# A hybrid attention and recurrence block: second copies of the values made on GpSimd, weight steps ahead of evictions, and the row of positions in free tiles

## The chip, the core and the metric

The kernel runs on one core of a Trainium2 chip. A core has five engines that run their own instruction streams and meet only at semaphores: TensorE (PE in the profile, its weight loads PEld) multiplies into PSUM, VectorE (DVE) and ScalarE (ACT) work elementwise on SBUF and PSUM, GpSimd (POOL) works on SBUF and issues DMAs, and SyncE (SP) issues DMAs. The metric is the device time of one execution in microseconds; less is better.

## What is computed

One block of a decoder over 1024 tokens of width 1024, all in float32: an RMS norm modulated by a condition vector, one input projection whose columns feed two branches, an attention over a sliding window of 128 with a learned sink per head, a gated linear recurrence behind a short convolution, the merge of both, an output projection and a final norm.

```python
h = rmsnorm(x, norm_g[l]) * (1.0 + scale[:, None, :]) + shift[:, None, :]
proj = h @ w_in[l]
q, k, v, g_attn, xr, g_rnn, m_attn, m_rnn = jnp.split(proj, SPLIT_POINTS, axis=-1)
q = partial_rope(q.reshape(B, S, N_HEADS, HEAD_DIM), positions)
k = partial_rope(k.reshape(B, S, N_KV_HEADS, HEAD_DIM), positions)
v = v.reshape(B, S, N_KV_HEADS, HEAD_DIM)
y_attn = sliding_window_attention_with_sinks(q, k, v, attn_sinks[l]) * jax.nn.silu(g_attn)
xr = causal_depthwise_conv(xr, conv_w[l], conv_b[l])
y_rnn = rg_lru(xr, positions, ...) * jax.nn.silu(g_rnn)
merged = (jax.nn.sigmoid(m_attn) * (y_attn @ w_attn_proj[l])
          + jax.nn.sigmoid(m_rnn) * (y_rnn @ w_rnn_proj[l]))
x = x + gate[:, None, :] * (merged @ w_out[l])
return rmsnorm(x, final_g)
```

## The kernel before

**Products.** Every float32 operand is split into a high part and a remainder, each in a form that TensorE multiplies at full rate, and a product is the sum of three (high by high, remainder by high, high by remainder). ScalarE makes the high part of a weight (`wh`, `cast`, line 104) and VectorE the remainder (`wl`, `rest`, line 110 or, with a scale, 112). The projection's columns are worked off in pairs of 128-column chunks by a scheme of Strassen's kind with seven products: `class Pair` holds one such pair, `product` (line 707) is one product of twelve matmuls, and a product fills one slot of the order.

**Order.** The instruction order of all engines is the order in which the Python code emits it. `Pair.place` enters a pair's steps into the list `fixed` by slot: loads of weights, their sums (`ws`, line 729), high parts and remainders ahead of the products that use them, and behind the products the evictions of the PSUM banks `bk`: copies by ScalarE (`u`, `p`, `bk`, lines 756 to 759), joins by VectorE (`c` or `xr`, line 767) and the sinks (`tanh_sinks`: a tanh on ScalarE, line 810, and for the SiLU gates a multiplication on VectorE, line 815). Two helpers enter steps: `at_slot` appends to a slot's list, `ahead` puts in front of what is there. The weight steps of a pair begin two slots before its first product, where the pair before it is being evicted. They are entered with `ahead` where the pair before is one of the queries (in `Q`), otherwise with `at_slot`, thus behind that pair's evictions. `run` walks over the slots, and `background` fills in the steps of the recurrence (`waiting`), whose scan is line 1064.

**The gate row.** `gate_row` (line 1092) reduces eight 128x1024 tiles of a weight with VectorE. A ninth tile of the same two buffers (`stage`) takes the row of positions, spread over 128 partitions, and line 1108 makes a reset mask (`rbig`) of it. The four tiles `wq` are not used until the output weights are prepared, behind the gate row.

**Attention.** The loop over `u` runs 35 iterations, each with one step of a software pipeline: scores of `u`, softmax of `u - 1`, transposes (`pt`), split (`phc` on ScalarE, `plc` on VectorE) and masks of `u - 2`, and the product with the values of `u - 3`. `masks` makes `cm` on GpSimd with two instructions, one for the upper 64 partitions from `phc`, one for the lower 64 from `plc` (line 1372); the last two matmuls of `values` read it in the next iteration (line 1386). Between these, `piece` emits a few matmuls of the rest of the projection and later of the recurrence branch's output projection (`rp`, line 175), so that TensorE has work while a softmax is under way. `sink` fills a column of the next score tile on GpSimd (`p`, line 1301).

**Values.** `load_v(m)` fills two tiles for two iterations, `vb` and `vd`, whose 128 partitions hold the values of 64 positions twice (for `vb` the second copy is one block on). Each is loaded in two halves by GpSimd's queue: four DMAs of 128 KB. It is called in `values` of an even iteration, two tiles ahead. The same queue carries the stores of the merge gates (`smr_d`), issued right behind their tanh. SyncE's queue carries the other loads of this stage, among them the recurrence branch's results `yh` and `yl`.

Of the kernel before, what the change touches and what calls it, by code (L numbers as in the profile page):

```python
# [12 lines left out]
F32 = mybir.dt.float32  # L13
F32R = mybir.dt.float32r
U32 = mybir.dt.uint32
I32 = mybir.dt.int32
BF16 = mybir.dt.bfloat16
AF = mybir.ActivationFunctionType
ALU = mybir.AluOpType
# [3 lines left out]
P = 128  # L23
S = 1024
D = 1024
KC = 8
# [26 lines left out]
def tile_hybrid_block(ctx, tc, x, x_t, pk, rows, posr, posi, c_row, w_ss, w_gate, w_main, w_v,  # L53
# [733 lines left out]
                "C21": lambda s: rope_b(s, 0, q_d[g]), "C22": (blk, lambda s: rope_b(  # L787
                    s, 1, q_d[g])), "late": 11}

    behind = []  # L790

    def store(dst, src):

# [9 lines left out]
    def tanh_sinks(dst, silu):  # L803
        def steps(j, th):
            def sink(s):
                t = {}

                def f1():
                    t["t"] = blk()
                    A.activation(t["t"], s(), AF.Tanh, scale=0.5)  # L810
                    if not silu:
                        dma(dst[j][:, SL[th]], t["t"], G)

                def f2():
                    V.scalar_tensor_tensor(out=t["t"], in0=t["t"], scalar=1.0, in1=s(),
                                           op0=ALU.add, op1=ALU.mult)
                    store(dst[j][:, SL[th]], t["t"])

                return [("A", 0.62, 0, f1)] + ([("D", 0, 0.69, f2)] if silu else [])
            return sink  # L820
        return {"C11": steps(0, 0), "C12": (blk, steps(0, 1)), "C21": steps(1, 0),
                "C22": (blk, steps(1, 1))}

    def place(pairs):
        for i, p in enumerate(pairs):
            p.place(7 * i, (i + len(pairs) + 1) % 2, i == len(pairs) - 1,
                    ahead if i and pairs[i - 1] in Q else at_slot)

    def run(pairs, extra):

# [261 lines left out]
    def gate_row():  # L1092
# [1 line left out]
        t = {}  # L1094

        def load(c):
            t[c] = gm.tile([P, D], F32 if c < KC else I32, tag="stage", name="wg", bufs=2)
            dma(t[c][:], w_gate[c * P:(c + 1) * P, :] if c < KC else posi.to_broadcast([P, S]))

        def start():  # L1100
            t["c"] = gm.tile([P, D], F32, name="cb")
# [3 lines left out]

        def step(c):
            if c == KC:
                V.tensor_scalar(out=rbig[:], in0=t[c][:], scalar1=0.0, scalar2=200.0,
                                op0=ALU.is_equal, op1=ALU.mult)
            else:  # L1110
                V.scalar_tensor_tensor(out=t[c][:], in0=t[c][:], scalar=0.25, in1=t["c"][:],
                                       op0=ALU.mult, op1=ALU.mult,
                                       accum_out=gate_bc[:, 0, c:c + 1])
# [43 lines left out]
        for c in range(KC + 1):  # L1157
            waiting[2].append([("D", 0, 1.28, lambda c=c: step(c))])
            if c + 2 <= KC:
                waiting[2].extend([slots(1), [("S", 0, 0, lambda c=c: load(c + 2))]])  # L1160
            waiting[2].extend(todo[c:c + 1] or [slots(1)])
        waiting[2].extend([[("D", 0, 0.1, out_row)], slots(6),
                           [("S", 0, 0, lambda: dma(
# [76 lines left out]

    at_ctx, psx_ctx = ExitStack(), ExitStack()
    at = psx = None
    U = {}

    def open_attn():
        nonlocal at, psx
# [35 lines left out]
    def load_v(m):  # L1282
        g, i0 = m // 4, m % 4 * 4
        vb = at.tile([P, 4, P], F32R, tag="vb", name="vb", bufs=3)
        vd = at.tile([P, 4, P], F32R, tag="vd", name="vd", bufs=3)
        for e in range(2):
            half = slice(64 * e, 64 * e + 64)
            dma(vb[half], vs_d[g][:, i0 + e:i0 + e + 4, :], G)
            dma(vd[half], dv_d[g][:, i0 + 2:i0 + 6, :], G)
        U["v", m] = vb, vd  # L1290

    def sink(u):
# [85 lines left out]
    def values(u):  # L1378
# [5 lines left out]
        for i, (b, m, h) in enumerate(prods):  # L1384
# [1 line left out]
            W["pe"] = T.matmul(pv[:, js, :], b[:, u % 2 * 2 + h, :], m[:, js, :],  # L1386
                               start=(i == 0), stop=(i >= len(prods) - 2),
                               skip_group_check=True)
        if u % 2 == 0 and u // 2 + 2 < 16:
            load_v(u // 2 + 2)  # L1390
        U["pv", u] = [pv[:].rearrange("p (h a) (e q) -> p a e h q", h=2, e=2)]

    def join_a(u):
# [284 lines left out]
    for u in range(32 + 3):  # L1678
# [31 lines left out]
            sink(u + 1)()  # L1710
        if 2 <= u < 34:
            masks(u - 2)
        if "hpool" in W:
            for f in low:
                f()
# [430 lines left out]
```

## Time and profile before

| what | before |
|---|---|
| runs | 905.7, 909.52, 909.77 us; median 909.52 |
| profiled execution | 906.86 us, of which the span 905.1 us |
| granted clock of TensorE | 0.998 of full speed |
| HBM read and written | 127.37 MB and 55.28 MB |

The span is the time from the first to the last instruction of one profiled execution; all positions below are microseconds from its start. A row of a timeline has the start, the length, the engine, the line and the operation, `out<-in` by the program's names. A matmul's length includes its way through the array, so that the rows of consecutive matmuls overlap. Idle time of an engine stands in brackets, with the instruction that ended it.

### The profile page before, as it was taken

What the parts mean: (1) busy time and instruction counts of PE and PEld (TensorE: products, weight loads), DVE (VectorE), ACT (ScalarE), POOL (GpSimd) and SP (SyncE); (2) the same over time, 40 slices, a digit from 0 to 9 for tenths busy, and PEclk for the clock granted to TensorE, in tenths of its full rate; (3) what the DMA queues carried; (4) which work ended last, traced back from release to release, by engine and by line L of the source; (5) the groups of instructions that cost most, each with busy time, mean ns of one, the idle gap of its engine ahead of it and who ended that gap; (6) DMA issues with size and microseconds to landing.
All of it is one profiled execution on the core that took longest, in us unless ns stands there. A gap on an engine that the chain in (4) does not pass through costs nothing.

```text
span 905.1 us, 12954 instructions
## 1 busy us (share of the span) xinstructions
PE 882.7 (98%) x4235; PEld 737.6 (81%) x4235; DVE 721.7 (80%) x1166; ACT 553.7 (61%) x1099; POOL 183.4 (20%) x309
## 2 busy tenths in 40 slices
PE   5999999999999999999999999998999999999997
PEld 3879888888888788878887888887888888888886
DVE  7988798888669974986698476898999846779875
ACT  6754675554566746674777685877888631114555
POOL 0130232210110000000100003565665421310002
PEclk9999999999999999999999999999999999999999
DMA  9951885972534451344244246899889369869314
GB/s 350 414 187 63 292 248 194 311 246 93 181 134 139 149 200 34 137 148 170 104 164 169 82 152 208 280 330 296 222 229 259 122 209 328 297 253 325 141 47 185
DMA packets 99445, 183.12 MB, mean 202 GB/s; under 512 B 31329, under 2 KB 44129, under 8 KB 99378
## 3 DMA queue, kind: packets, MB, share of 16 engines
q1 hardware_dynamic: 86912, 144.52, 47.1%
q0 software_dynamic: 12176, 37.47, 12.5%
q8 instruction: 33, 0.54, 0.2%
q10 hardware_dynamic: 290, 0.32, 0.1%
q14 instruction: 34, 0.28, 0.1%
HBM read 127.37 MB, written 55.28 MB: 202 GB/s over the span
## 4 chain that ended last, share of the span: by engine, by line
PE 70%; DMA 11%; issue 8%; DVE 5%; ACT 4%; POOL 2%; SPq 0%; DVEq 0%; POOLq 0%; ACTq 0%
PE bk L707 39%; PE bo L1918 8%; PE rp L175 7%; PE pgate L1003 5%; DMA yl<-yl_d 3%; PE pmain L175 2%; PE s_ps L1317 2%; DMA r<-w_main 2%; PE pv L1386 2%; DMA wq<-w_out 2%; DMA hl<-yl_d 1%; DMA wq_d<-wq 1%; PE pt L1354 1%; PE bk L175 1%; DVE wl L110 1%
## 5 line engine op out<-in xcount | busy, mean ns | idle before, releaser
L707 PE MATMUL bk<-nh,wl 128*128 128x512 f32 x368 | 143.7, 390 | 0.4 <-DVE wl L110 0.4
L707 PE MATMUL bk<-nh,wh 128*128 128x512 f32 x368 | 143.3, 390 | 0.0
L707 PE MATMUL bk<-nl,wh 128*128 128x512 f32 x368 | 143.2, 389 | 0.0
L707 PEld LDWEIGHTS bk<-nh,wl 128*128 128x128 f32 x368 | 69.1, 188 | 16.1 <-DVE wl L110 1.9
L110 DVE TENSOR_TENSOR wl<-r,wh 128x512 fp32r<-128x512 f32 x112 | 81.4, 740 | 0.0
L707 PEld LDWEIGHTS bk<-nh,wh 128*128 128x128 f32 x368 | 69.1, 188 | 14.4
L707 PEld LDWEIGHTS bk<-nl,wh 128*128 128x128 f32 x368 | 69.1, 188 | 14.1
L60 POOL DMA_DIRECT2D wq_d<-wq x32 | 21.9, 684 | 270.4 <-DVE wq L1191 255.4
L104 ACT CAST wh<-r 128x512 fp32r<-128x512 f32 x112 | 68.0, 617 | 9.0 <-DMA r<-w_ap 6.3
L707 PE MATMUL bk<-hh,wl 128*128 128x512 f32 x184 | 71.7, 390 | 0.1
L707 PE MATMUL bk<-hh,wh 128*128 128x512 f32 x184 | 71.6, 389 | 0.0
L707 PE MATMUL bk<-hl,wh 128*128 128x512 f32 x184 | 71.6, 389 | 0.0
L110 DVE TENSOR_TENSOR wl<-ws,wh 128x512 fp32r<-128x512 f32 x80 | 54.5, 684 | 4.2 <-ACT wh L104 4.2
L1340 ACT ACTIVATE p<-p,small 128x129 f32<-128x129 f32 x128 | 50.1, 401 | 0.0
L104 ACT CAST wh<-ws 128x512 fp32r<-128x512 f32 x80 | 48.2, 614 | 2.9 <-PE bk L1570 2.7
L810 ACT ACTIVATE c<-bk 128x512 f32<-128x512 f32 x31 | 18.5, 597 | 44.3 <-PE bk L707 42.3
L707 PEld LDWEIGHTS bk<-hh,wl 128*128 128x128 f32 x184 | 34.5, 188 | 7.7 <-DVE wl L112 0.5
L707 PEld LDWEIGHTS bk<-hh,wh 128*128 128x128 f32 x184 | 34.6, 188 | 7.2
L707 PEld LDWEIGHTS bk<-hl,wh 128*128 128x128 f32 x184 | 34.5, 188 | 7.0
L1918 PE MATMUL bo<-wh,sum 128*128 128x512 f32 x128 | 39.6, 389 | 0.0
L1317 PE MATMUL s_ps<-ks,qs 128*128 128x192 f32 (+2 forms) x256 | 35.5, 281 | 2.1 <-DMA qs<-q_d 1.4
L707 PE MATMUL bk<-hha,wl 128*128 128x512 f32 x92 | 36.0, 392 | 0.6 <-DVE wl L110 0.6
(420 smaller groups left out, 2336.5 us busy)
## 6 DMA issues: line engine op xcount, KB each, us to landing
r<-w_main SPq DMA_DIRECT2D x100, 256.0 KB, 4.2
wada<-w_ss SPq DMA_DIRECT2D x16, 512.5 KB, 9.2
wq_d<-wq POOLq DMA_DIRECT2D x24, 256.0 KB, 3.0
wr<-wq_d SPq DMA_DIRECT2D x24, 256.0 KB, 4.8
ks<-k_d SPq DMA_DIRECT2D x24, 192.0 KB, 3.5
wg<-w_gate SPq DMA_DIRECT2D x8, 512.0 KB, 6.2
sma_d<-c POOLq DMA_DIRECT2D x16, 256.0 KB, 3.9
sgr_d<-c SPq DMA_DIRECT2D x16, 256.0 KB, 2.2
```

The lines of the kernel that those rows point to most:

```text
L60: return eng.dma_start(dst, src)
L104: A.copy(dst[0][:], src)
L110: V.tensor_tensor(out=dst[1][:], in0=src, in1=f32(dst[0][:]), op=ALU.subtract)
L175: mm = T.matmul(ps[hf], ww, xx[kc][hf], start=(kc == first and ww is w_h and xx is xh), stop=(kc == last and xx is xl))
L707: W["pe"] = T.matmul(ps, ww[:, c], b[kc][xx_], start=(first and kc == 0 and i == 0), stop=(kc == 3 and i == 2), skip_group_check=not first)
L810: A.activation(t["t"], s(), AF.Tanh, scale=0.5)
L1003: W["pe"] = T.matmul(ps[:, SL[hf]], ww[:, c0:c0 + P], xx_[:, SL[hf]], start=(ic == 0 and i == 0), stop=(ic == 1 and i == 2))
L1317: W["pe"] = T.matmul(s_ps[:, j, first:192], w, ks[:, b, t0 + first:t0 + 192], start=(b == 0), stop=(b == 1))
L1340: A.activation(px[:, j, :], px[:, j, :], AF.Exp, bias=sm[:, 0, j:j + 1], accum_out=sm[:, 1, j:j + 1])
L1354: W["pe"] = T.transpose(pt[:, j, :], px[:, j, 0:P], ident[:])
L1386: W["pe"] = T.matmul(pv[:, js, :], b[:, u % 2 * 2 + h, :], m[:, js, :], start=(i == 0), stop=(i >= len(prods) - 2), skip_group_check=True)
L1918: T.matmul(bank[p][i] if dst is None else dst, a[:, ts_], b[:][:, sl], start=(new and kc == 0 and j == 0), stop=(kc == 3 and j == 2), skip ...
```

## The change

It has four parts. First, in `place`, the weight steps of a pair that does not follow a query pair go to `next_`: the first step is appended as before, the later ones go ahead of what stands in their slots. Second, from the third tile on, `load_v` loads one half of `vb` and `vd` and one block of the other half of `vb` (32 KB); the rest of the second halves is copied by two GpSimd instructions, emitted behind the masks of iteration `2m + 1`. Third, `load_v` is called behind the masks, one iteration earlier, and within attention the stores of the merge gates are kept in `tail` and issued behind the masks too. Fourth, the row of positions is loaded in two halves into two of the tiles `wq`, and the reset mask is made in two halves.

```diff
-    behind = []
+    behind, tail = [], []
...
                     if not silu:
-                        dma(dst[j][:, SL[th]], t["t"], G)
+                        tail.append(lambda: dma(dst[j][:, SL[th]], t["t"], G))
+                        if "att" not in W:
+                            tail.pop()()
...
+    def next_(t, *steps):
+
+        at_slot(t, *steps[:1])
+        ahead(t + 1, *steps[1:])
+
     def place(pairs):
         for i, p in enumerate(pairs):
             p.place(7 * i, (i + len(pairs) + 1) % 2, i == len(pairs) - 1,
-                    ahead if i and pairs[i - 1] in Q else at_slot)
+                    ahead if i and pairs[i - 1] in Q else next_ if i else at_slot)
...
+        def row():
+            for i in range(2):
+                t[KC, i] = wq[i][:].rearrange("p a t -> p (a t)").bitcast(I32)
+                dma(t[KC, i], posi[:, SL[i]].to_broadcast([P, HALF]))
...
-                V.tensor_scalar(out=rbig[:], in0=t[c][:], scalar1=0.0, scalar2=200.0,
-                                op0=ALU.is_equal, op1=ALU.mult)
+                for i in range(2):
+                    V.tensor_scalar(out=rbig[:, SL[i]], in0=t[c, i], scalar1=0.0, scalar2=200.0,
+                                    op0=ALU.is_equal, op1=ALU.mult)
...
+            if c == 3:
+                waiting[2].append([("S", 0, 0, row)])
...
-        for e in range(2):
-            half = slice(64 * e, 64 * e + 64)
-            dma(vb[half], vs_d[g][:, i0 + e:i0 + e + 4, :], G)
-            dma(vd[half], dv_d[g][:, i0 + 2:i0 + 6, :], G)
+        a, b = slice(0, 64), slice(64, 128)
+        dma(vb[a], vs_d[g][:, i0:i0 + 4, :], G)
+        dma(vd[a], dv_d[g][:, i0 + 2:i0 + 6, :], G)
+        if m < 2:
+            dma(vb[b], vs_d[g][:, i0 + 1:i0 + 5, :], G)
+            dma(vd[b], dv_d[g][:, i0 + 2:i0 + 6, :], G)
+        else:
+            dma(vb[b, 3, :], vs_d[g][:, i0 + 4, :], G)
+            twice.setdefault(2 * m + 1, []).extend([
+                lambda: G.tensor_copy(vb[b, 0:3, :], vb[a, 1:4, :]),
+                lambda: G.tensor_copy(vd[b], vd[a])])
...
-        if u % 2 == 0 and u // 2 + 2 < 16:
-            load_v(u // 2 + 2)
...
             masks(u - 2)
+        for f in twice.pop(u, []) + tail:
+            f()
+        tail.clear()
+        if u >= 2 and u % 2 == 0 and u // 2 + 1 < 16:
+            load_v(u // 2 + 1)
```

TensorE's stream is the same, row by row. On VectorE, between two pairs (beside the recurrence's scan, near 305 us in the profile), `c<-c,bk` and `c<-u,bk` are evictions of the old pair, `wl` and `ws` belong to the next weights. Before:

```order
L1064 SCALAR_TENSOR_TENSOR rz<-av,it 128x1024
L815 SCALAR_TENSOR_TENSOR c<-c,bk_68 128x512
L767 TENSOR_TENSOR c<-u_3082,bk_71 128x512
L110 TENSOR_TENSOR wl<-r,wh 128x512
L729 TENSOR_TENSOR ws<-ws,r 128x512
L767 TENSOR_TENSOR c<-bk_69,p_3034 128x512
L110 TENSOR_TENSOR wl<-ws,wh 128x512
```

And now:

```order
L1071 SCALAR_TENSOR_TENSOR rz<-av,it 128x1024
L110 TENSOR_TENSOR wl<-r,wh 128x512
L729 TENSOR_TENSOR ws<-ws,r 128x512
L817 SCALAR_TENSOR_TENSOR c<-c,bk_68 128x512
L767 TENSOR_TENSOR c<-u_3083,bk_71 128x512
L110 TENSOR_TENSOR wl<-ws,wh 128x512
L729 TENSOR_TENSOR ws<-r 128x512
```

Two evictions have moved behind the remainder of the next weight and behind one sum.

On GpSimd, at the start of attention (near 571 to 579 us in the profile), `cm` are the masks, `p<-sink` fills the sink column, `smr_d<-c` is a store of a merge gate, `vb` and `vd` are loads of values. Before:

```order
L1372 AFFINE_SELECT cm<-phc 64x512
L1372 AFFINE_SELECT cm<-plc 64x512
L60 DMA smr_d_120<-c 128x512
L60 DMA vb<-vs_d_89 64x512
L60 DMA vd<-dv_d_93 64x512
L60 DMA vb<-vs_d_89 64x512
L60 DMA vd<-dv_d_93 64x512
L1301 COPY p<-sink 128x4
L1372 AFFINE_SELECT cm<-phc 64x512
L1372 AFFINE_SELECT cm<-plc 64x512
L1301 COPY p<-sink 128x4
```

And now, up to the copies of the first tile that has them:

```order
L60 DMA vb<-vs_d_89 64x512
L60 DMA vd<-dv_d_93 64x512
L60 DMA vb<-vs_d_89 64x128
L1324 COPY p<-sink 128x4
L1395 AFFINE_SELECT cm<-phc 64x512
L1395 AFFINE_SELECT cm<-plc 64x512
L60 DMA smr_d_120<-c 128x512
L1324 COPY p<-sink 128x4
L1395 AFFINE_SELECT cm<-phc 64x512
L1395 AFFINE_SELECT cm<-plc 64x512
```

The store stands behind the next masks. The loads keep their place between the masks of an even iteration and the fill of the next one, since they are emitted an iteration earlier but at its end; there are three instead of four. The copies come two iterations later:

```order
L1324 COPY p<-sink 128x4
L1395 AFFINE_SELECT cm<-phc 64x512
L1395 AFFINE_SELECT cm<-plc 64x512
L1311 COPY vb<-vb 64x384
L1312 COPY vd<-vd 64x512
L60 DMA smr_d_120<-c 128x512
```

They stand behind the masks of an odd iteration, and 14 tiles have them.

More of the change, by code (lines that the diff above doesn't have):

```diff
@@ L1096, in load @@
         def load(c):
-            t[c] = gm.tile([P, D], F32 if c < KC else I32, tag="stage", name="wg", bufs=2)
-            dma(t[c][:], w_gate[c * P:(c + 1) * P, :] if c < KC else posi.to_broadcast([P, S]))
+            t[c] = gm.tile([P, D], F32, tag="stage", name="wg", bufs=2)
+            dma(t[c][:], w_gate[c * P:(c + 1) * P, :])
+        def row():
+            for i in range(2):
+                t[KC, i] = wq[i][:].rearrange("p a t -> p (a t)").bitcast(I32)
+                dma(t[KC, i], posi[:, SL[i]].to_broadcast([P, HALF]))
         def start():
@@ L1159, in gate_row @@
             if c + 2 <= KC:
-                waiting[2].extend([slots(1), [("S", 0, 0, lambda c=c: load(c + 2))]])
+                waiting[2].extend([slots(1), [("S", 0, 0, lambda c=c: load(c + 2) if c + 2 < KC
+                                               else None)]])
+            if c == 3:
+                waiting[2].append([("S", 0, 0, row)])
             waiting[2].extend(todo[c:c + 1] or [slots(1)])
@@ L1242, in tile_hybrid_block @@
     at = psx = None
-    U = {}
+    U, twice = {}, {}
     def open_attn():
```

## The prediction

> **What bounds the kernel now.** I read the busy shares first, then who made TensorE wait, then the stages in which it waited, and last the instructions around each wait. Busy shares:
>
> ```profile
> PE 882.7 (98%) x4235; PEld 737.6 (81%) x4235; DVE 721.7 (80%) x1166; ACT 553.7 (61%) x1099; POOL 183.4 (20%) x309
> ```
>
> Of the span of 905.1 us TensorE is idle for 905.1 - 882.7 = 22.4 us. That is all that any reordering can win, since the change leaves TensorE's own instructions and their order alone. Here is every stop of TensorE between 50 and 890 us, in time order (start, length, operation, in brackets the idle time ahead of it and who ended it):
>
> ```profile
> 308.90 0.50 PE L707 MATMUL bk<-hha,wl 128*128 128x512 f32 x1 [0.41 <-DVE wl L110]
> 396.45 0.50 PE L707 MATMUL bk<-hha,wl 128*128 128x512 f32 x1 [0.21 <-DVE wl L110]
> 489.93 0.50 PE L707 MATMUL bk<-nh,wl 128*128 128x512 f32 x1 [0.37 <-DVE wl L110]
> 578.97 0.50 PE L1386 MATMUL pv<-cm,vd 128*128 128x256 f32 x2 [0.72 <-POOL cm L1372]
> 594.27 0.51 PE L1386 MATMUL pv<-cm,vd 128*128 128x256 f32 x2 [0.37 <-POOL cm L1372]
> 600.66 1.14 PE L1317 MATMUL s_ps<-ks,qs 128*128 128x192 f32 x8 [0.66 <-DVE p L1333]
> 616.89 1.11 PE L1317 MATMUL s_ps<-ks,qs 128*128 128x192 f32 x8 [1.41 <-DMA qs<-q_d]
> 621.50 0.73 PE L175 MATMUL rp<-yl,wh 128*128 128x512 f32 x2 [1.14 <-DMA yl<-yl_d]
> 718.07 0.50 PE L1386 MATMUL pv<-cm,vd 128*128 128x256 f32 x2 [0.36 <-POOL cm L1372]
> 800.65 0.73 PE L175 MATMUL rp<-ah,wl 128*128 128x512 f32 x2 [0.16 <-DVE wl L110]
> ```
>
> They sum to 5.81 us; the other 16.6 us lie in the first 50 and the last 25 us, where the change does nothing. So **5.8 us, 0.64% of the time, is the ceiling**. Most of it is in one stretch, seen in the busy time of each engine by stage (TensorE, its loads, DVE, ACT, POOL, then clock, share of the DMA engines, GB/s):
>
> ```profile
> 580.00:600.00 20.00, 19.58 (x119) 16.98 (x118) 17.12 (x32) 17.31 (x56) 13.13 (x25) 1.00 1.01 304
> 600.00:620.00 20.00, 17.93 (x106) 15.53 (x106) 19.27 (x37) 15.90 (x53) 12.41 (x20) 1.00 1.05 320
> 620.00:640.00 20.00, 18.86 (x119) 16.68 (x118) 15.97 (x32) 15.23 (x50) 10.78 (x21) 1.00 0.96 259
> 640.00:700.00 60.00, 60.00 (x375) 53.51 (x374) 55.73 (x107) 51.20 (x167) 35.55 (x63) 1.00 0.88 239
> ```
>
> In the first part of attention the DMA engines are full (1.01, 1.05), and VectorE is at 96% from 600 to 620. From 640 to 700 TensorE never stops, so nothing can be won there, only lost.
>
> **Pairs: next weight's steps first.** At 308.90 VectorE ran these ahead of the weight's remainder:
>
> ```profile
> 306.98 0.66 DVE L815 SCALAR_TENSOR_TENSOR c<-c,bk 128x512 f32<-128x512 f32 x1
> 307.56 0.68 DVE L767 TENSOR_TENSOR c<-u,bk 128x512 f32<-128x512 f32 x1
> 308.16 0.69 DVE L110 TENSOR_TENSOR wl<-r,wh 128x512 fp32r<-128x512 f32 x1
> 311.54 0.39 PE L707 MATMUL bk<-nh,wh 128*128 128x512 f32 x1
> ```
>
> The two evictions take 308.16 - 306.98 = 1.18 us and now stand behind wl, so the wait of 0.41 goes; 396.45 has the same three operations and its 0.21 goes too: **-0.62 us**. At 489.93 wl follows a scan that keeps its place, so 0.37 stays:
>
> ```profile
> 487.01 2.29 DVE L1064 TENSOR_TENSOR_SCAN rz<-av,it 128x1024 f32<-128x1024 f32 x1
> 489.21 0.67 DVE L110 TENSOR_TENSOR wl<-r,wh 128x512 fp32r<-128x512 f32 x1
> ```
>
> The price is an eviction 1.2 to 1.4 us later, on a bank that TensorE writes again. In the place quoted, c<-u,bk ended at 308.24, and the next product that starts its bank anew began at 311.54: 3.3 us of slack, 1.9 left. I take 0; were that cover gone, each of the 19 affected pairs could lose what the eviction exceeds it by. On ScalarE one tanh of 0.6 us moves behind one cast, with the same cover. **The row of positions**: one integer operation becomes two halves, and the load is asked for earlier; VectorE's wait for it is not TensorE's, for no stop stands near it. 0.
>
> ```profile
> DVE rbig L1108 <- DMA wg<-posi: 1.8, 1, 1.8
> ```
>
> **Masks ahead of GpSimd's issues.** At 578.97 the queue on GpSimd had been:
>
> ```profile
> 574.18 0.56 POOL L60 DMA_DIRECT2D smr_d<-c  x1 [1.82 <-ACT c L810]
> 574.74 0.53 POOL L60 DMA_DIRECT2D vb<-vs_d  x1
> ...
> 576.89 0.19 POOL L1301 COPY p<-sink 128x4 f32<-128x4 f32 x1
> 577.03 0.65 POOL L1372 TENSOR_SCALAR_AFFINE_SELECT cm<-phc 64x512 fp32r<-64x512 f32 x1
> 577.74 1.17 POOL L1372 TENSOR_SCALAR_AFFINE_SELECT cm<-plc 64x512 fp32r<-64x512 f32 x1
> 575.58 0.69 DVE L1365 TENSOR_TENSOR plc<-pt,phc 128x512 fp32r<-128x512 f32 x1
> 587.19 1.09 DVE L110 TENSOR_TENSOR wl<-r,wh 128x512 fp32r<-128x512 f32 x1
> ```
>
> A store waited 1.82 us for ScalarE at the head, four issues followed, then the masks. In the new order the store stands behind both masks, and three issues (of which one is a quarter of the size) start when the previous mask ends. The masks then start when their inputs are there; VectorE's plc was done at 576.27, so cm is ready near 577 and the 0.72 goes. At 594.27 cm was late because VectorE was: one iteration before, its wl sat from 587.19 for 1.09 us beside the phc mask, instead of 0.68. With that mask earlier wl gains 0.41, and the 0.37 goes. Together **-1.09 us, but only if nothing later swallows it**. The wait at 718.07 is for VectorE's plc itself and stays. The moved stores are read only in the merge behind attention, so none of them can be late.
>
> **Second copies by GpSimd.** For 14 of 16 loads, 128 + 96 = 224 KB no longer come by DMA; instead GpSimd copies 64x384 and 64x512. No such copy is in the trace. GpSimd's nearest rows are the masks above (64x512, one in, one out: 0.65) and, to either side, a fill and a two-input operation:
>
> ```profile
> L1299 POOL MEMSET p<- 128x256 f32 x4 | 1.3, 314 | 0.2
> L2033 POOL TENSOR_TENSOR r<-r,fg_bc 128x512 f32<-128x512 f32 x2 | 2.6, 1308 | 0.0
> ```
>
> So 0.3 to 1.3 us each; I take the mask's 0.65 and three quarters to all of it, 0.55: 1.2 us every second iteration. GpSimd has the room (35.55 of 60 us). The first and the last of four loads that the DMA engines had to serve between 580 and the stop at 621.50, and the size of one piece:
>
> ```profile
> 584.84 0.53 POOL L60 DMA_DIRECT2D vb<-vs_d  x1
> ...
> 614.01 0.52 POOL L60 DMA_DIRECT2D vb<-vs_d  x1
> vb<-vs_d POOLq DMA_DIRECT2D x32, 128.0 KB, 4.5
> ```
>
> 224 KB at the 304 to 320 GB/s above is 0.72 us, so with four of them the yl that ended that stop can land up to 2.9 us sooner. Not all of it comes through, since the queue that asks for yl also waits for TensorE (SyncE from 575 to 640: total, times, longest):
>
> ```profile
> SPq L60 <- PE s_ps L1317: 14.4, 4, 5.2
> ```
>
> I take three quarters, 2.2 us. yl decides: without the stops of 0.72, 0.37, 1.41 and 1.14 TensorE would reach that matmul 3.6 us earlier than 621.50, yl allows 2.2. So the stretch gives **-2.2 us** and the gain of the masks is inside it. I leave the 0.66 at 600.66, which ends on VectorE at its fullest (19.27 of 20 us): that the copies of that iteration cost it about the 0.41 which wl saved is assumed, with 0 and 1.2 us as the ends.
>
> **The sum.** -0.62 - 2.2 = -2.8 us. The profiled execution took 906.86 us (span 905.1 plus 1.76 around it), so 904.0. The three timed runs were 905.7, 909.52 and 909.77: their median stands 2.66 above the profiled one, the mean of all four (907.97) 1.1 above. A median may fall in either group, so I put the forecast between 904.0 and 906.7: **905.4 us**.
>
> **Rivals.**
>
> *DMA relief frees the whole stretch.* If yl lands 3.6 us or more sooner, all of 0.72 + 0.37 + 0.66 + 1.41 + 1.14 = 4.30 goes, with 0.62 that is 4.92: 901.9 us. For it: the stretch is the one place where the DMA share exceeds 1, and the runs that took 2.7 us more may have lost it there. Against it: 2.9 us is all that the removed bytes come to.
>
> *The relief does not reach yl.* If its request is held by TensorE and not by the engines, yl lands when it did, and only the pairs' 0.62 is left: 906.2 us.
>
> *VectorE becomes the bound.* In a steady iteration its remainder of a weight ran beside a mask:
>
> ```profile
> L110 DVE TENSOR_TENSOR wl<-r,wh 128x512 fp32r<-128x512 f32 x7 | 8.0, 1136 | 0.0
> L1365 DVE TENSOR_TENSOR plc<-pt,phc 128x512 fp32r<-128x512 f32 x13 | 9.0, 692 | 0.4
> ```
>
> All 7 between 640 and 700 us take 1136 ns, where the row at 308.16 has 0.69: 0.45 lost to GpSimd. VectorE has 60 - 55.73 = 4.27 us free over 13 iterations, 0.66 per two. If the 1.2 us of copies blocked it for their whole length, it would be over by 0.54 us per two iterations, 14 times: 7.6 us, less the 2.8 won: 911.7. It decides above 0.66 us blocked per load. Against it, where the copies would fall:
>
> ```profile
> 668.69 0.98 POOL L1372 TENSOR_SCALAR_AFFINE_SELECT cm<-plc 64x512 fp32r<-64x512 f32 x1 [0.26 <-DVE plc L1365]
> 670.44 0.69 DVE L1347 TENSOR_TENSOR p<-p,small 128x512 f32<-128x512 f32 x1
> 671.77 0.42 DVE L1410 TENSOR_TENSOR rbig<-pv,ob 64x256 f32<-64x256 f32 x1 [0.64 <-ACT ob L1398]
> ```
>
> Copies would run from 669.67 to 670.87 and hold up p<-p,small by 0.43, ahead of 0.64 in which VectorE idles anyway. The Trainium skill, "SBUF — State Buffer", "Who interferes with whom", says that a VectorE instruction with two SBUF inputs and a GpSimd instruction that reads SBUF shut each other out, and that whichever issues second blocks fully. The 1136 ns agree. By that rule alone each copy could hold VectorE for its full length, the 911.7 above.
>
> **Chances.** Forecast (gain 1 to 4.5) 0.45; whole stretch freed 0.26; no relief 0.18; VectorE bound 0.11. About 0.5%, 4.5 us, is what a measurement of this kernel can tell from no change. The second case is faster by that, or nearly, and the forecast is so at its edge: faster 0.29. Most of the last case is slower: 0.08. Same: 0.63. The range goes from just below the freed stretch, 901.5, to the no-relief case against the higher runs (906.2 + 2.7 = 908.9) and a little of the last, 909.5.
>
> **What would show it.** Right: no stop left near 308, 396 and 579; the one at 621 shorter or gone, with the DMA share of 580 to 620 below 1; copies of 0.5 to 0.7 us. Wrong: new stops of TensorE from 640 to 700, VectorE's p<-p,small near 1.1 us instead of 0.69, a bk product that waits for an eviction, or yl landing as late after its request as before.

## The result, and the profile after

| what | before | after |
|---|---|---|
| median of 9 runs each (lowest to highest) | 909.52 us (905.7 to 912.67) | 901.38 us (899.68 to 904.57) |
| ratio, 95% interval | | 0.9917, 0.9894 to 0.9941 |
| profiled execution, its span | 906.86 us, 905.1 us | 901.38 us, 899.7 us |
| TensorE idle within the span | 22.4 us | 19.2 us |

The kernel became 0.83% faster. By medians that is 8.1 us, by the two profiled executions 5.5. Busy time by engine after:

```profile
PE 880.5 (98%) x4235; PEld 738.1 (82%) x4235; DVE 722.8 (80%) x1167; ACT 555.1 (62%) x1099; POOL 193.8 (22%) x323
```

TensorE runs the same 4235 matmuls, and yet its busy time is 2.2 us less, beside the 3.2 us of idle time that went. GpSimd has 10.4 us more: 18.6 of copies, less the issues that they replace. All stops of TensorE over 0.15 us between 50 and 890 us, as they were listed for before:

```profile
309.16 0.50 PE L707 MATMUL bk<-hha,wl 128*128 128x512 f32 x1 [0.29 <-DVE wl L110]
591.70 0.50 PE L1409 MATMUL pv<-cm,vd 128*128 128x256 f32 x2 [0.26 <-POOL cm L1395]
597.48 0.51 PE L1409 MATMUL pv<-cm,vd 128*128 128x256 f32 x2 [0.74 <-POOL cm L1395]
616.57 0.73 PE L175 MATMUL rp<-yl,wh 128*128 128x512 f32 x2 [0.80 <-DMA yl<-yl_d]
713.22 0.50 PE L1409 MATMUL pv<-cm,vd 128*128 128x256 f32 x2 [0.37 <-POOL cm L1395]
```

2.46 us are left of 5.81. The stops at 578.97 and 600.66 and the one for `qs` (1.41) are gone, and the one for `yl` is shorter. Counted by the order of TensorE's matmuls, the stop at 591.70 is the one at 594.27 before, and 713.22 is 718.07; the stop at 597.48 is new. The stages of the first part of attention (TensorE, its loads, DVE, ACT, POOL, clock, DMA share, GB/s):

```profile
580.00:600.00 20.00, 19.00 (x119) 16.77 (x118) 18.02 (x36) 17.37 (x57) 15.66 (x27) 1.00 0.98 334
600.00:620.00 20.00, 19.20 (x120) 16.86 (x119) 19.00 (x36) 16.02 (x53) 12.86 (x23) 1.00 1.05 306
620.00:640.00 20.00, 20.00 (x126) 17.86 (x125) 18.15 (x35) 16.88 (x56) 13.58 (x25) 1.00 0.71 201
640.00:700.00 60.00, 60.00 (x374) 53.49 (x373) 55.93 (x108) 50.72 (x169) 40.65 (x71) 1.00 0.80 225
```

The DMA engines are about as full as before until 620 and much less after it (0.71 instead of 0.96). From 640 to 700 TensorE never stops, with 5.1 us more of GpSimd's work beside it: nothing was lost there. The copies, and the division by the softmax's sum that they were expected to hold up (line, engine, operation, count, busy time, mean ns of one; the copies over the whole run, the division from 635 to 695 us):

```profile
L1311 POOL CAST vb<-vb 64x384 fp32r<-64x384 f32 x14 | 9.6, 689 | 0.0
L1312 POOL CAST vd<-vd 64x512 fp32r<-64x512 f32 x14 | 9.0, 641 | 0.0
L1370 DVE TENSOR_TENSOR p<-p,small 128x512 f32<-128x512 f32 x12 | 8.6, 713 | 0.4
```

**Where the time went.** TensorE's instructions stand in the same order in every kernel here, so the start of the n-th one can be compared between two traces. The table gives by how much TensorE gained (-) or lost (+) against before within four stretches, named by the positions of before: 90 to 221 us holds the row of positions, 221 to 558 the pairs, 558 to 642 the first part of attention, 642 to 822 the rest of it. The first 25 us are left out: no part of the change touches them, and they differ by -0.1 to +2.0 us between these executions. One trace stands for each kernel, so a few tenths in a cell are no finding. In the first column -0.4 is the level of a kernel without a stop there, because before lost that much near 139 us in its own trace. The losses of 0.34 to 1.35 in the last column are one stop near 800 us (`rp<-ah,wl`, 0.56 to 1.51 us, 0.16 in before); why only some kernels have it was not looked into and stays open.

| kernel | ratio to before (95%) | 90-221 | 221-558 | 558-642 | 642-822 |
|---|---|---|---|---|---|
| the change | 0.9917 (0.9894 to 0.9941) | +0.05 | -1.49 | -3.74 | -0.36 |
| pairs_only | 0.9979 (0.9957 to 1.0002) | -0.40 | -1.54 | -1.25 | -0.42 |
| copies_only | 0.9961 (0.9939 to 0.9983) | +1.26 | +0.64 | -3.58 | +1.04 |
| order_only | 1.0010 (0.9996 to 1.0025) | -0.41 | +0.01 | +3.31 | -0.13 |
| att_only (copies, order) | 1.0016 (0.9998 to 1.0034) | -0.41 | +0.50 | +0.79 | -0.36 |
| att_turned | 0.9988 (0.9973 to 1.0002) | -0.37 | +0.02 | +1.27 | +0.34 |
| row_only | 1.0034 (1.0015 to 1.0054) | +2.73 | +0.52 | +0.88 | +1.35 |
| no_order | 0.9925 (0.9897 to 0.9953) | +1.63 | -1.55 | -4.35 | -0.45 |
| no_copies | 1.0005 (0.9985 to 1.0024) | +2.02 | -2.13 | +3.24 | -0.42 |
| no_row | 0.9912 (0.9884 to 0.9940) | +0.25 | -1.52 | -4.66 | -0.44 |
| pairs_copies | 0.9920 (0.9894 to 0.9946) | +0.67 | -2.12 | -4.32 | +0.50 |
| copies_twice | 0.9918 (0.9886 to 0.9950) | +0.28 | -1.92 | -4.46 | -0.52 |
| row_late | 0.9904 (0.9883 to 0.9926) | -0.41 | -1.71 | -4.64 | -0.51 |

So the change wins in the stretch of the pairs and, most of all, in the first part of attention. In the trace of before, one row already says why the idle column counts too little. These are the neighbours of its stop at 396.45, which the list of before gives as 0.21:

```profile
395.86 0.39 PE L707 MATMUL bk<-hha,wh 128*128 128x512 f32 x1
...
396.79 0.39 PE L707 MATMUL bk<-hla,wh 128*128 128x512 f32 x1
397.02 0.40 PE L707 MATMUL bk<-hha,wh 128*128 128x512 f32 x1
```

The same matmuls after:

```profile
396.10 0.39 PE L707 MATMUL bk<-hha,wh 128*128 128x512 f32 x1
396.33 0.39 PE L707 MATMUL bk<-hha,wl 128*128 128x512 f32 x1
396.56 0.39 PE L707 MATMUL bk<-hla,wh 128*128 128x512 f32 x1
```

After, the starts are 0.23 apart. Before, 396.45 - 395.86 = 0.59 and then 0.34: 0.36 + 0.11 = 0.47 us lost for an idle time of 0.21, because the matmul ahead counts as busy for 0.39 us while its successor would normally start after 0.23.

### The profile page after: what moved, and what is told of

It is laid out like the page before. It is cut to its first block, busy times and chain, and to the rows that moved or that the text cites. A ratio compares the mean times of both kernels' runs of the same rounds, so it can differ in the third digit from the quotient of the medians.

```text
span 899.7 us, 12984 instructions
## 1 busy us (share of the span) xinstructions
PE 880.5 (98%) x4235; PEld 738.1 (82%) x4235; DVE 722.8 (80%) x1167; ACT 555.1 (62%) x1099; POOL 193.8 (22%) x323
## 4 chain that ended last, share of the span: by engine, by line
PE 87%; DMA 5%; DVE 3%; ACT 2%; issue 1%; SPq 1%; POOL 0%; DVEq 0%; ACTq 0%
PE bk L707 47%; PE rp L175 12%; PE bo L1944 8%; PE pmain L175 6%; PE pgate L1010 5%; DMA yl<-yl_d 3%; PE s_ps L1340 2%; PE pv L1409 2%; PE pt L1377 1%; PE bk L175 1%; DMA hl<-yl_d 1%; DMA r<-w_main 1%; PE bk L1591 1%; PE bk L1590 1%; PE bk L1589 1%
## 5 line engine op out<-in xcount | busy, mean ns | idle before, releaser
L707 PE MATMUL bk<-hla,wh 128*128 128x512 f32 x92 | 35.8, 389 | 0.0
```

Of the source, the lines that this page charges most:

```text
L707: W["pe"] = T.matmul(ps, ww[:, c], b[kc][xx_], start=(first and kc == 0 and i == 0), stop=(kc == 3 and i == 2), skip_group_check=not first)
```

## The experiments

Each was timed against the kernel before on the same chip. They stand in four groups: the parts alone, the parts left out, GpSimd's room, and the two waits that the first runs brought to light.

### The parts alone

**pairs_only**, against the kernel before:

```diff
+    def next_(t, *steps):
+        at_slot(t, *steps[:1])
+        ahead(t + 1, *steps[1:])
...
-                    ahead if i and pairs[i - 1] in Q else at_slot)
+                    ahead if i and pairs[i - 1] in Q else next_ if i else at_slot)
```

> The kernel before with next_ alone (next weight's steps ahead of evictions). Theory A: the idle time of TensorE in the records understates a stop, since a matmul's modelled length covers the first part of it; the starts of the matmuls tell it. Then the starts at the first score product (558.1 us before) come 1.4 us earlier against the starts near 90 us, as in the changed kernel, and the whole time falls by about 1.4 us. Rival: only the visible idle of 0.41 + 0.21 goes, 0.6 us, and the rest of that shift belongs to another part of the change. The stops at 578, 616 and 621 us stay.

Measured: 908.15 us, ratio 0.9979; its interval reaches just above 1, so the time alone does not show the gain. By the starts it is there: from 221 to 558 TensorE gains 1.54 us, as in the whole change. It also gains 1.25 in attention, where the part changes no order: the stop of 0.66 at 600 fell to 0.37 and those for `qs` and `yl` to 1.05 and 0.57.

**copies_only**, against the kernel before: the new body of `load_v`, called where it was, and the copies behind the masks.

```diff
+            dma(vb[b, 3, :], vs_d[g][:, i0 + 4, :], G)
+            twice.setdefault(2 * m + 1, []).extend([
+                lambda: G.tensor_copy(vb[b, 0:3, :], vb[a, 1:4, :]),
+                lambda: G.tensor_copy(vd[b], vd[a])])
...
             masks(u - 2)
+        for f in twice.pop(u, []):
+            f()
```

> The kernel before with second copies by GpSimd, loads called and stores issued where they were. Theory A (DMA relief): yl lands 2 us or more earlier, the starts from 640 us on are 2 to 3 us earlier, and the stop of 0.72 at 579 is still there. Theory B (order): the starts from 640 us on are within 1 us of before.

Measured: 906.54 us, ratio 0.9961. The stretch 558 to 642 gains 3.58 us: no stop for `qs` or `yl` is left, and not even the one of 0.72 at 579, though the masks still stand behind the issues. Of what it lost elsewhere, 1.26 us come from a stop that before did not have (the rest stands at two later stops for a `wl`, at 311 and 800 us):

```profile
207.82 0.69 DVE L1108 TENSOR_SCALAR rbig<-wg 128x1024 bf16<-128x1024 int32 x1 [3.36 <-DMA wg<-posi]
209.17 0.50 PE L707 MATMUL bk<-nh,wl 128*128 128x512 f32 x1 [1.27 <-DVE wl L110]
```

The row of positions is still loaded late here. VectorE waited 3.36 us for it instead of 1.85, and the weight's remainder behind it stopped TensorE for 1.27.

**order_only**, against the kernel before: stores into `tail`, `load_v` behind the masks.

```diff
             masks(u - 2)
+        for f in tail:
+            f()
+        tail.clear()
+        if u >= 2 and u % 2 == 0 and u // 2 + 1 < 16:
+            load_v(u // 2 + 1)
```

> The kernel before with only the order on GpSimd changed: loads of values called at the end of an even iteration, stores of merge gates behind the masks, all four loads as DMAs, no copies. Theory A (relief of the DMA engines is what lets yl come sooner): the stop of 0.72 at 579 goes, the stop for yl near 621 stays or grows, and the starts from 640 us on are no more than 0.5 us earlier. Theory B (the queue of requests was held by the late masks, and the order alone frees it): the starts from 640 us on are 3 us or more earlier, as in the changed kernel (3.7).

Measured: 911.44 us, ratio 1.0010, no different from before by its interval, but with 3.31 us lost in attention, which neither theory expected. The two rows that explain it, and the stores on GpSimd's queue:

```profile
593.69 1.10 POOL L60 DMA_DIRECT2D smr_d<-c  x2
602.99 0.69 DVE L1542 TENSOR_TENSOR al<-rbig,ah 128x512 fp32r<-128x512 f32 x1 [5.96 <-issue]
605.30 2.02 PE L1319 MATMUL s_ps<-ks,qs 128*128 128x192 f32 x8 [5.44 <-DVE p L1335]
```

`al` lies in a pool that is opened when the pool of the five `c` tiles, out of which the merge gates are stored, has been closed. By the program's semaphores it waits for the second of the last two stores. That store now stands behind two masks, is issued near 594.2 and lands 8.7 us later. VectorE stands still for 5.96 us, and the scores behind it stop TensorE for 5.44. In before the same store was issued at 591.02, and `al` waited for 0.45:

```profile
591.02 0.55 POOL L60 DMA_DIRECT2D smr_d<-c  x1 [0.81 <-ACT c L810]
597.95 1.08 DVE L1542 TENSOR_TENSOR al<-rbig,ah 128x512 fp32r<-128x512 f32 x1 [0.45 <-issue]
```

The stop also cost what its idle time does not contain: behind it the granted clock (third figure from the end) fell to half.

```profile
605.00:610.00 5.00, 4.70 (x15) 4.12 (x16) 4.82 (x10) 3.92 (x13) 2.52 (x4) 0.50 1.00 337
```

Until about 611 us the matmuls `rp` start 0.43 us apart instead of 0.23, and TensorE falls another 2.6 us behind. Part of all this is won back, because the loads of `qs` and `yl` are there when TensorE comes to them.

**att_only**: copies and order together, the two diffs above joined in one line.

```diff
+        for f in twice.pop(u, []) + tail:
+            f()
```

> Both GpSimd parts together (copies, loads at the end of an even iteration, stores behind the masks) on the kernel before, without the pairs and the row of positions. Both theories: the starts from 640 us on 3.7 us earlier, and the profiled time about 4 us lower. For the medians, which moved by 8.1 us where the profiled runs moved by 5.4: if runs of the kernel before lose more in the crowded start of attention than the profiled one did, this kernel's median falls by 6 us or more; if that excess lies elsewhere, by about 4.

Measured: 911.22 us, ratio 1.0016; the gain that was expected did not come. The copies' gain is eaten by the same wait, and by 1.6 us of slow matmuls behind it (clock 0.66 from 605 to 610):

```profile
602.94 0.69 DVE L1549 TENSOR_TENSOR al<-rbig,ah 128x512 fp32r<-128x512 f32 x1 [4.70 <-issue]
605.25 1.84 PE L1326 MATMUL s_ps<-ks,qs 128*128 128x192 f32 x8 [4.54 <-DVE p L1342]
```

**row_only**, against the kernel before:

```diff
+        def row():
+            for i in range(2):
+                t[KC, i] = wq[i][:].rearrange("p a t -> p (a t)").bitcast(I32)
+                dma(t[KC, i], posi[:, SL[i]].to_broadcast([P, HALF]))
...
+            if c == 3:
+                waiting[2].append([("S", 0, 0, row)])
```

> The kernel before with the row of positions loaded in two halves into free tiles, alone. Theory A: the load of the row lands at a time that differs between executions (VectorE waited 1.3, 1.5, 1.8, 2.9 and 3.4 us for it in the five profiles that have it), and beyond about 2 us it holds TensorE (1.27 us idle at 209 us in the run with 3.4). Then this kernel's median falls by 0.5 to 1.5 us, and no stop stands near 209 us. Rival: the wait is VectorE's alone, and the time stays within 0.3 us. The profile may show a gain or none, as the load fell in the profiled run.

Measured: 912.57 us, ratio 1.0034: slower by itself, where a gain or nothing was expected, with 2.73 us lost between 90 and 221. SyncE's queue, VectorE and TensorE there:

```profile
170.21 1.71 SPq L60 DMA_DIRECT2D wq<-posi  x2
171.97 4.01 SPq L60 DMA_DIRECT2D r<-w_main  x2
181.34 0.69 DVE L729 TENSOR_TENSOR ws<-r 128x512 f32<-128x512 f32 x1 [5.39 <-DMA r<-w_main]
182.69 0.50 PE L707 MATMUL bk<-nh,wl 128*128 128x512 f32 x1 [1.69 <-DVE wl L112]
```

The row's 512 KB now stand ahead of the next two loads of `w_main`. Before had these at 169.81, and VectorE waited for them much less:

```profile
169.81 1.26 SPq L60 DMA_DIRECT2D r<-w_main  x2
176.53 0.69 DVE L729 TENSOR_TENSOR ws<-r 128x512 f32<-128x512 f32 x1 [0.89 <-DMA r<-w_main]
```

### The parts left out

**no_order**: the change with `tail` and the moved call of `load_v` taken back.

```diff
-        for f in twice.pop(u, []) + tail:
+        for f in twice.pop(u, []):
             f()
-        tail.clear()
-        if u >= 2 and u % 2 == 0 and u // 2 + 1 < 16:
-            load_v(u // 2 + 1)
```

> The changed kernel without its order on GpSimd: pairs, row and copies stay, loads are called and stores issued where they were before. Theory A: the order costs on its own (a large stop near 605 us in the two runs that had it without the pairs, where VectorE's first remainder into a new tile waits for the last stores to land, because that tile lies on their buffers), and is worth 1 us at most where it does not; then this kernel is within 1.5 us of the changed one (901.4), and it shows the stop of 0.7 at 577. Rival: order and copies together are what frees the start of attention, and this kernel loses 3 us.

Measured: 902.83 us, ratio 0.9925, the same as the change within the intervals. The stretch of attention gains 4.35 us without the new order of GpSimd: that part of the change is worth nothing here.

**no_copies**: the change with the old body of `load_v`.

```diff
+        for e in range(2):
+            half = slice(64 * e, 64 * e + 64)
+            dma(vb[half], vs_d[g][:, i0 + e:i0 + e + 4, :], G)
+            dma(vd[half], dv_d[g][:, i0 + 2:i0 + 6, :], G)
```

> The changed kernel without the copies: all four loads are DMAs; pairs, row and order stay. Theory A (the pairs decide which of five rotating buffers the last stores use, so that the remainder's tile lies on another): there is no stop near 603 us, and what is lost against the changed kernel is the relief of the DMA engines, 2 to 3.5 us, seen as a stop for qs or yl of 1 us or more. Rival (the order without copies makes the stores late by itself): a stop of 4 us or more for VectorE near 603 us, as in the run with the order alone.

Measured: 910.34 us, ratio 1.0005. All of the gain is gone. The expected loss against the change was 2 to 3.5 us; it is 7.0 in the stretch of attention, -3.74 against +3.24. Most of it is one stop for `qs`, behind which the clock fell to 0.52 (620 to 625 us) and another 2.4 us went:

```profile
619.56 0.71 PE L1333 MATMUL s_ps<-ks,qs 128*128 128x192 f32 x2 [4.11 <-DMA qs<-q_d]
```

`al` waits for nothing here, so without the copies the new order seems to have a second price: pairs_only, which has neither the order nor the early row and loads as much by DMA, gains 1.25 us in this stretch. Why `qs` is so late was not shown.

**pairs_copies**: the diffs of pairs_only and of copies_only together. **no_row**: the change without the row's part.

```diff
-            if c == 3:
-                waiting[2].append([("S", 0, 0, row)])
```

> Pairs and copies alone, neither the row nor GpSimd's order. If the parts add up (pairs alone 0.9979, copies alone 0.9961): 0.994, 904 us. Theory (no_order, the same with the row, gave 0.9925; the row costs 0 to 2 us): 0.9905 to 0.9925, 900.5 to 902.8 us; a masks' stop of 0.3 to 0.7 us near 595 stays, no yl stop over 0.6 us. Rival (the row is worth 1 to 2 us): 0.9935 to 0.9945.

> The whole change without the part of the row. Theory (the row is worth nothing or costs up to 2 us): the wait for r near 178 is 0.5 to 1.5 us, rbig waits 1 to 3.4 us near 205 with a stop of 0 to 1.3 us behind it, al waits under 1 us since the pairs have turned the ring; ratio 0.990 to 0.9925. Rival (the row is a gain of 1 to 2 us): ratio 0.9928 to 0.994.

Measured: 901.75 us (ratio 0.9920) and 900.6 us (0.9912). Pairs and copies alone give the whole gain, and more than the two alone would add up to (0.9979 x 0.9961 = 0.994; the intervals of the two readings touch). With the row or without it, with the order or without it: 0.9912 to 0.9925, which no run here tells apart. In no_row the row of positions is late again, 3.72 us of VectorE's time, of which 0.36 reach TensorE.

### GpSimd's room

**copies_twice**: the change with each copy made a second time.

```diff
                 lambda: G.tensor_copy(vd[b], vd[a]),
+                lambda: G.tensor_copy(vb[b, 0:3, :], vb[a, 1:4, :]),
+                lambda: G.tensor_copy(vd[b], vd[a])])
```

> The changed kernel with GpSimd making the copy of vb a second time behind the two copies (an extra 64x384 copy, or two, each of 0.5 to 0.95 us, in every second iteration of attention). Theory A: GpSimd's and VectorE's room hides the copies, and the time rises by less than 0.7 us in all. Rival (the shared port, by which VectorE's two-input operations block): VectorE's p<-p,small goes to 1 us or more in those iterations, and TensorE stops from 640 to 700 us, 0.3 us or more for each of 14 tiles: 4 us.

Measured: 901.9 us, ratio 0.9918, no different from the change. In the steady part GpSimd is at 50.27 of 60 us and TensorE still never stops:

```profile
640.00:700.00 60.00, 60.00 (x376) 53.64 (x376) 56.01 (x108) 50.83 (x169) 50.27 (x84) 1.00 0.80 226
```

VectorE's busy time rose by 0.08 us only (55.93 to 56.01): the copies hold up hardly any of its instructions, and the rows under **The rivals** below show why.

### The two waits

**row_late**: the change, the row asked for behind the last load of `w_gate`.

```diff
-            if c == 3:
+            if c == 5:
                 waiting[2].append([("S", 0, 0, row)])
```

> The whole change, the row's two loads issued after step 5 of the gate's rows (behind the last load of w_gate) instead of after step 3 (ahead of the next two loads of w_main). Theory (the early row holds up the loads of w_main behind it: VectorE waited 4.4 us for r at 178 in the changed kernel, 0.9 before, and with 5.0 to 5.4 us TensorE stopped for 1.1 to 1.7 us at 182): the wait for r near 178 is 0.5 to 1.5 us, no TensorE stop near 182, rbig waits for nothing, the time is 0.3 to 2.5 us below that of the changed kernel, ratio 0.989 to 0.9914. Rival (that wait is inside VectorE's slack in the whole change): ratio 0.9917 as in the changed kernel, within 0.001. Second rival (the row is late again): rbig waits over 1 us and a stop of bk at 205.

Measured: 901.13 us, ratio 0.9904. Both waits are gone or small, and no TensorE stop over 0.15 us is left between 50 and 590 us:

```profile
176.65 0.69 DVE L729 TENSOR_TENSOR ws<-r 128x512 f32<-128x512 f32 x1 [1.27 <-DMA r<-w_main]
204.12 0.75 DVE L1121 TENSOR_SCALAR rbig<-wq 128x512 bf16<-128x512 int32 x2
```

In the changed kernel the first of these waited 4.44 us. So the early row does hold up `w_main`. In the time it shows as 0.5 us in the stretch 90 to 221 of these two traces; the ratios (0.9904 and 0.9917) lie within each other's intervals.

**att_turned**: att_only, with two small memsets of `c` tiles ahead of everything, so that the ring of five stands two further.

```diff
+    for _ in range(2):
+        V.memset(blk()[0:1, 0:8], 0.0)
```

> Copies and GpSimd's order alone (as att_only: 911.22, ratio 1.0016), with two 1x8 memsets of `c` tiles ahead of the first use of that pool, so that the ring of its five buffers stands two further at every later use and VectorE's first `al` no longer lies on the tiles of the last two smr_d stores. Theory (what order costs without the pairs is only the accident of which buffer lies under `al`): the idle time of 4.7 us ahead of `al` near 602 is under 1.5 us, the s_ps stop of 1.84 us at 605 is gone, the starts from 640 on stand 4 to 6 us earlier than in att_only against 558, the time is 905.5 to 907.5 (ratio 0.9945 to 0.998). Rival (the late stores and loads themselves crowd the DMA, and something else then waits there): another stop of 1 us or more between 595 and 625, time 909.5 to 912, ratio over 0.999.

Measured: 908.65 us, ratio 0.9988: outside what the theory expected, and outside the rival's too.

```profile
593.00 1.10 POOL L60 DMA_DIRECT2D smr_d<-c  x2
...
600.19 0.69 DVE L1552 TENSOR_TENSOR al<-rbig,ah 128x512 fp32r<-128x512 f32 x1 [4.14 <-issue]
602.50 2.03 PE L1329 MATMUL s_ps<-ks,qs 128*128 128x192 f32 x8 [3.68 <-DVE p L1345]
```

The turn by two did not free `al`: by the semaphores it now waits for the first of the last two stores instead of the second. It starts 7.2 us after that one's issue, and the stop is 0.86 us shorter than in att_only. The clock fell behind this stop too (0.63 from 605 to 610), which cost another 2.8 us. A ring in which `al` lies on neither was not tried by itself. What stands behind the cause is the comparison of all kernels with the new order: where `al` waits for one of the last two stores (order_only, att_only, att_turned) the stop is 5.44, 4.54 and 3.68 us; where it waits only for earlier ones (the change, no_row, row_late, copies_twice, no_copies) `al` waits for nothing. In those five the pairs had moved the order in which the `c` tiles are taken; in pairs_only too, which may be why its stop of 0.66 at 600 shrank. The row of the change:

```profile
594.57 0.68 DVE L1563 TENSOR_TENSOR al<-rbig,ah 128x512 fp32r<-128x512 f32 x1
```

## Why the prediction was right in its direction and short in its size

**The forecast.** 905.4 was 4.0 us too high, and 901.38 lies 0.12 below the low end of the range. The mechanism that was named, DMA relief in the first part of attention and weights ahead of evictions, is the one that acted (pairs_only and copies_only show each by itself). The term that failed in size is the relief by the second copies, put at 2.2 us with 2.9 as the most, and measured at 3.74; the pairs were put at 0.62 and gave 1.5. Two prices that were set to nothing, of the later evictions and of the early row, are not nothing, and the 0.66 at 600.66 that was left in the sum went.

**"So 5.8 us is the ceiling"** fell. From 90 to 822 us the change gains 0.26 + 5.28 = 5.5 us, and no_row 6.4, while only 3.35 us of the listed idle time went. The listed idle time is too small a measure of a stop, as the rows at 396 show, and busy time fell too (882.7 to 880.5).

**Pairs, -0.62.** The place was right, the size was not: 1.5 us in the change and in pairs_only. Of the three stops the one at 396.45 went. Between 390 and 402 us the change gains 0.71 by the starts: the 0.47 worked out above, and most of the rest at 399.39, where before lost 0.2 without any idle time in the list. The one at 489.93 was to stay "behind a scan that keeps its place" and went, since VectorE, with its joins behind the weight, came to the scan at 486.04 instead of 487.01. The one at 308.90 was to go and stayed as 0.29, and this is where the later evictions have a price after all. They did move behind the weight, but the scan ahead of it came 1.45 us later (TensorE itself was 0.38 us later by then). In before (ScalarE: a tanh that needs a join, then the recurrence's tanh; VectorE: the scan):

```profile
290.62 0.63 ACT L810 ACTIVATE c<-c 128x512 f32<-128x512 f32 x1 [1.23 <-DVE c L767]
...
300.45 1.06 ACT L1052 ACTIVATE th<-th 128x1024 f32<-128x1024 f32 x1
304.78 2.28 DVE L1064 TENSOR_TENSOR_SCAN rz<-av,it 128x1024 f32<-128x1024 f32 x1
```

After, with the join and the scan on VectorE:

```profile
292.15 0.68 DVE L767 TENSOR_TENSOR c<-bk,p 128x512 f32<-128x512 f32 x1
292.87 0.63 ACT L810 ACTIVATE c<-c 128x512 f32<-128x512 f32 x1 [1.80 <-DVE c L767]
...
301.90 1.06 ACT L1059 ACTIVATE th<-th 128x1024 f32<-128x1024 f32 x1
306.23 2.29 DVE L1071 TENSOR_TENSOR_SCAN rz<-av,it 128x1024 f32<-128x1024 f32 x1
308.43 0.67 DVE L110 TENSOR_TENSOR wl<-r,wh 128x512 fp32r<-128x512 f32 x1
```

The join, now behind the weight, holds up the gate's tanh on ScalarE, behind it stand the recurrence's steps, behind these the scan, and behind the scan the next weight. The prediction looked for the price in the banks, and there it was right: no product waits for an eviction in the list after.

**The row of positions, 0.** The number held, its reason did not. "VectorE's wait for it is not TensorE's" was true of 1.85 us in one execution; with 3.36 us in copies_only it stopped TensorE for 1.27 (with the pairs moved, 3.72 in no_row and 4.00 in pairs_copies cost 0.36 and 0.64). And the load that was moved had a price on SyncE's queue that the prediction did not work out: it now stands ahead of `w_main`, whose wait grew from 0.89 to 4.44 us, and to 5.39 with a stop of 1.69 in row_only. One wait was traded for the other; row_late, which has neither, shows that the trade was not necessary.

**Masks ahead of issues, -1.09 inside the stretch.** The stop at 579 went, but copies_only has none there without this part either. The stop at 594 stayed, as 0.26 at 591.70: the `wl` that was blamed for it did shrink, to 0.68 at 585.04, but the mask at 590.66 still waited 0.42 for VectorE's plc. And the order made a new stop, 0.74 at 597.48:

```profile
591.60 1.09 POOL L60 DMA_DIRECT2D smr_d<-c  x2
...
596.43 0.99 POOL L1395 TENSOR_SCALAR_AFFINE_SELECT cm<-plc 64x512 fp32r<-64x512 f32 x1
```

VectorE's plc was done at 594.65. Two stores and three loads, issued behind one iteration's masks, now stood ahead of the next one's, so "the masks then start when their inputs are there" failed. All five kernels with pairs and order have this stop (0.70 to 0.97), and no other kernel has it. The other sentence that failed is "none of them can be late": the data of the moved stores are read late, but their buffers are wanted early, by `al`. Without the pairs that costs 0.5%, the slower clock behind the stop included (att_only 1.0016 against copies_only 0.9961); with them the ring happens to stand right.

**Second copies, -2.2 for the stretch.** The copies took 0.69 + 0.64 = 1.33 us per load, where 1.2 was estimated. The term was mis-sized: 3.74 us, and 3.58 to 4.66 in all the kernels with copies but without the wait of `al`. The cut to three quarters was made because SyncE's queue also waits for TensorE; the request for the `yl` that decides did not. The last two requests for `yl` in before, and after:

```profile
597.01 0.32 SPq L60 DMA_DIRECT2D yl<-yl_d  x1
609.36 0.58 SPq L60 DMA_DIRECT2D yl<-yl_d  x1
```

```profile
591.69 0.39 SPq L60 DMA_DIRECT2D yl<-yl_d  x1
603.82 0.33 SPq L60 DMA_DIRECT2D yl<-yl_d  x1
```

The first of each two took 12.3 and 12.1 us to land, and the second was issued 0.02 us after that: by the program's semaphores a transfer of SyncE's queue waits until the eighth before it in this queue has landed. The second took 12.1 us in before and 12.7 after. So what the prediction named as a sign of being wrong, yl landing as late after its request as before, came true. The relief did not shorten that load. It came through earlier loads: the `hl` whose landing let the first `yl` go took 12.7 us before (asked for at 584.33) and 8.9 after (582.75). The request came 5.54 us sooner, of which 1.2 were there at 558 already, and the matmul that needs it 4.93 us sooner, still behind a wait of 0.80, so yl is the last to be late, as the prediction said. In copies_only yl took 10.5 us and landed 3.6 us sooner than in before, though that kernel was 2.3 us late at 558: 5.9 us of relief, twice what the removed bytes were put at. Why a byte taken off was worth that much stays open. Of the other signs, the DMA share below 1 held from 580 to 600 only (0.98, then 1.05).

**The rivals.** "DMA relief frees the whole stretch" (4.30 us, 901.9 us) came nearest in time: its condition was met (yl 4.93 us sooner), with 3.74 in the change, and 4.3 to 4.7 in the five kernels with pairs and copies in which yl does not stop TensorE. "The relief does not reach yl" fell. "VectorE becomes the bound" fell: with twice the copies nothing is lost. The rule of the Trainium skill, "SBUF — State Buffer", "Who interferes with whom", that a VectorE instruction with two SBUF inputs and a GpSimd instruction that reads SBUF shut each other out, is not refuted by that. Where a `wl`, which has two inputs, had begun, the vb copy took 0.94 us, and `wl` no longer than the 1.14 of before:

```profile
674.11 1.13 DVE L110 TENSOR_TENSOR wl<-r,wh 128x512 fp32r<-128x512 f32 x1
674.67 0.94 POOL L1311 CAST vb<-vb 64x384 fp32r<-64x384 f32 x1
```

In the other iterations the vb copy ran beside `small<-p`, a reduction with one input, and took 0.50 (at 683.95). Only p<-p,small was held up, by 0.08 us in 3 of 13 instances between 640 and 700, where 0.43 had been read off the rows. So the copies mostly did not meet two-input instructions of VectorE, or waited themselves.

**The base.** The sum was made against one execution of 906.86 us, at the low end of the runs of before (905.7 to 912.67). The medians differ by 2.7 us more than the two profiled executions. What the longer runs of before lose was not profiled, and stays open.

## What to carry to other kernels

Measure a stop by the distance of the starts of consecutive matmuls, against their usual one, and compare traces with the same instruction order start by start; idle time in brackets gave less than half of what 396.45 cost. When a store is moved later, ask who next takes its buffer, not only who reads its data; when a load is moved earlier, ask what stands behind it in its queue. Where the DMA engines are full, take bytes off them first: the copies made most of the gain here, and the new order of GpSimd's queue was worth nothing beside them and, where `al` fell on the last stores, cost their gain.

## What the runs showed of the hardware that was not expected

- The matmul after a stop takes 0.50 us instead of 0.39, and its successor starts 0.34 us later instead of 0.23 (396.45 and 396.79 of before), so that a stop costs about 0.1 us behind itself.
- Behind stops of 3.7 to 5.4 us the granted clock fell to 0.50 to 0.66 over 5 us (order_only, att_only, att_turned, no_copies), the matmuls started 0.43 us apart instead of 0.23, and TensorE lost another 1.6 to 2.8 us. Behind stops of up to 1.76 us (row_only) the clock from 600 to 640 stayed at 1.00.
- With the DMA share near 1, a store of 256 KB was done 7.2 us (att_turned) and 8.7 us (order_only) after its issue, judged by the start of the instruction that waited for it; a load of `yl` (512 KB) took 12.1 to 12.7 us.
- In the first 25 us, which all these kernels share, the executions differ by up to 2.1 us at the same instruction, a quarter of the change's whole effect.
